# A decoder trunk on one core: a fourth seven-product block in each feed-forward layer, and the output pieces moved

## The chip, the core and the metric

The kernel runs on one core of one Trainium2 chip. The metric is device time in microseconds, measured over the whole launch. The median of three runs of the kernel before is 1028.6 us (1028.21, 1028.6 and 1033.28).

## The reference

The kernel computes a small decoder trunk for 256 tokens of width 1024: two layers, each with a feed-forward layer, a mixer and another feed-forward layer, and a residual with LayerNorm after each. The first mixer is a sparse attention, the second a state-space scan. The change touches the four feed-forward layers alone:

```python
D_MODEL = 1024
SEQ = 256
D_FF = 2816

def swiglu_ffn(x, w_in, w_out):
    gate, up = jnp.split(x @ w_in, 2, axis=-1)
    return (jax.nn.silu(gate) * up) @ w_out

# for each of the two layers i
x = layer_norm(DEEPNORM_ALPHA * x + 0.5 * swiglu_ffn(x, ffn1_w_in[i], ffn1_w_out[i]), ...)
m = mixer(x)
x = layer_norm(DEEPNORM_ALPHA * x + m, ...)
x = layer_norm(DEEPNORM_ALPHA * x + 0.5 * swiglu_ffn(x, ffn2_w_in[i], ffn2_w_out[i]), ...)
```

## The kernel before, in words

**Numbers.** Every operand of a large product is held as two halves: a rounded high part (H) and the rest, the low part (L). A product is three matmuls, H by H, H by L and L by H (`mm3`, L534 to L537).

**Weights.** The host cuts all weights into tiles of 128 x 1024 numbers (512 KB) and lays them in one array in the order of their use. A planner, the class `Weights` (L209), loads them in that order through SP's queue (`load`) and turns each into a unit, a high part by ScalarE (`make`, L329) and a low part by VectorE (`lows`, L357). At most ten units exist at once (`SLOTS`), and 7 or 9 raw tiles (`W.raws`). The order of the instructions on each engine is the order in which the program writes them. Each step of the program calls `pump` (L371), which makes up to n more units. VectorE's work is kept as a debt in columns (`owe`), and each product of TensorE takes 2400 off it (`product`, L263). Above a debt of 2500 (`MOST`), `pump` goes on only until the made units are six ahead of the used ones.

**A feed-forward layer** (`ffn`, L740). The 2816 gate columns and 2816 up columns are cut into 22 column blocks of 128 each, numbered j = 0 to 21. One layer goes through these parts:

- *Wide* (blocks 0 to 3): for both halves of the tokens, gate and up columns of two blocks are one product of 512 columns with the tokens on the output's partitions. Results lie in banks from `pmm()` (two banks in turn), in the first layer of the kernel the second pair in banks from `ptr()` (two in turn). `glu` (L775) takes silu of the gate half on ScalarE, and VectorE multiplies by the up half, which it reads in PSUM. `tr` (L764) then transposes on TensorE, ScalarE rounds (hH, L772) and VectorE splits off the low part (hL, L773).
- *One-block steps* (`one`, L872), R4 to R7: one column block at a time, a projection for the gate and one for the up columns (`proj_w`, lines L684 and L686), with the columns on the partitions, so that no transposes are needed.
- *Seven-product blocks* (`seven`, L903), S8, S12 and S16: four column blocks at once. The tokens are cut in two halves and the 1024 inputs in two halves, which makes a 2 x 2 by 2 x 2 block product; it is done with seven products in place of eight (A11, Q1, Q4, S2, S3, A12, A22), each four `mm3` of 512 columns. For this some weight tiles are added to others first (`sum`), by VectorE (L296) or by an accumulating DMA that POOL issues (L269), and so are input halves (`XT.sums`, L557, eight steps). ScalarE copies partial results out of PSUM and VectorE combines them; then comes `glu` as above.
- R20 and R21, one-block steps again.
- *Output pieces* (`out_pieces`, L848): one row block of the second weight matrix for all tokens, twelve matmuls into four banks (`acc`). Piece j can come when the hidden block j is split. Before, pieces 0 and 1 follow R6 and R7; four each lie in the slots of S8, S12 and S16; 14 and 15 follow R20 and R21.
- *Tail* (L695): the last six pieces, 16 to 21, for the first token half and then for the second, with the two LayerNorms.

Work that must wait is put off by steps: `later(f, d)` queues f for the d-th step from now, and `step` runs what is due and then pumps.

`ffn_steps` (L69) is the list of these parts, from which both the host's order of the weights (`ffn_units`, L83) and the device program are made.

Of the kernel before, what the change touches and what calls it, by code (L numbers as in the profile page):

```python
# [10 lines left out]
F32 = mybir.dt.float32  # L11
# [10 lines left out]
NJ = FF // 128  # L22
# [39 lines left out]

WIDE = 2
LAG = 6
SEVEN = (8, 12, 16)
MOST = 2500


def ffn_steps():  # L69


    steps, j, o = [], 2 * WIDE, 0
    while j < NJ:
        kind, n = ('S', 4) if j in SEVEN else ('R', 1)
        j += n
        outs = list(range(o, min(o + 4, max(o, j - LAG))))
        o += len(outs)
        steps.append((kind, j - n, outs))
    assert o == NJ - LAG, o
    return steps  # L80


def ffn_units(ws, wi, wo, wide, lag):  # L83
    def colblk(c0):
        return wi[:, c0:c0 + 128]

    def ktile(blk):
        n = blk.shape[1]
        return blk.reshape(DK, 128, n).transpose(1, 0, 2)

    def out_unit(j):
        ws.append(wo[j * 128:(j + 1) * 128])

    for w in range(wide):
        j = 2 * w
        blk = np.concatenate([wi[:, j * 128:(j + 2) * 128], wi[:, FF + j * 128:FF + (j + 2) * 128]], axis=1)
        t = ktile(blk)
        for k in range(0, DK, 2):
            ws.append(t[:, k:k + 2].reshape(128, -1))
    def quarter(j, kh):  # L100

        blk = np.concatenate([wi[:, j * 128:(j + 2) * 128], wi[:, FF + j * 128:FF + (j + 2) * 128]], axis=1)
        t = ktile(blk)
        return [t[:, k:k + 2].reshape(128, -1) for k in (4 * kh, 4 * kh + 2)]

    for kind, j, outs in ffn_steps():
        if kind == 'S':
            outs = outs + [None] * (4 - len(outs))

            def out():  # L110
                o = outs.pop(0)
                if o is not None:
                    out_unit(o)

            b11 = [ws.append(a) for a in quarter(j, 0)]
            b12 = [ws.raw(a) for a in quarter(j + 2, 0)]
            for i in range(2):
                ws.sum(b11[i], b12[i])
            out()
            b22 = [ws.append(a) for a in quarter(j + 2, 1)]  # L120
            for i in range(2):
                ws.sum(b11[i], b22[i])
            out()
            for i in range(2):
                ws.sum(b12[i], b22[i], True)
            b21 = [ws.append(a) for a in quarter(j, 1)]
            out()
            for i in range(2):
                ws.sum(b11[i], b21[i], True)
            out()  # L130
        else:
            ws.append(ktile(colblk(j * 128)).reshape(128, -1))
            ws.append(ktile(colblk(FF + j * 128)).reshape(128, -1))
            for o in outs:
                out_unit(o)
    for j in range(NJ - lag, NJ):
        out_unit(j)
# [276 lines left out]
def trunk_kernel(ctx: ExitStack, tc: tile.TileContext, widths, forms, x, ln_g, ln_b, wts, kvg, convp,  # L414
                 dt_bias, a_log, d_skip, norm_g, out):
    nc = tc.nc
# [5 lines left out]
    psum = ctx.enter_context(tc.tile_pool(name="psum", bufs=1, space=bass.MemoryType.PSUM))  # L422
# [4 lines left out]
    def nm(s):  # L427
        cnt[0] += 1
        return f"{s}_{cnt[0]}"
# [32 lines left out]
    def ptr():  # L462
        return psum.tile([128, 512], F32, name=nm("ptr"), tag="ptr", bufs=2)
# [276 lines left out]
    def ffn(xT, u0, ln_i, first=False, last=False, ff=False):  # L740
# [9 lines left out]
        def later(f, d=1):  # L750

            while len(queue) < d:
                queue.append([])
            queue[d - 1].append(f)
# [8 lines left out]

        def tr(t, w, h):  # L764

            pt = psum.tile([128, 512], F32, name=nm("pht"), tag=f"acc1{t}", bufs=1) if w < WIDE else ptr()
            for i in range(2):
                nc.tensor.transpose(pt[:, i * 128:(i + 1) * 128], h[:, i * 128:(i + 1) * 128], ident)
            v = pt[:, :256].rearrange("p (j t) -> p j t", j=2)
            sl = (slice(None), slice(None), slice(t * 128, (t + 1) * 128))  # L770
            H, L = [a[w].rearrange("p (j t) -> p j t", j=2)[sl] for a in (hH, hL)]
            nc.scalar.copy(H, v)  # L772
            return lambda: nc.vector.tensor_sub(L, v, H.bitcast(F32))  # L773

        def glu(t, w, c, sil=None):  # L775


            g, h = (c[:, :256], c[:, 256:]) if sil is None else (sil, f1("h"))
            nc.scalar.activation(g, c[:, :256], AF.Silu)

            def mul():
                nc.vector.tensor_mul(h, c[:, 256:], g)
                W.owe(800)
                later(lambda: later(tr(t, w, h)), 4 if w < WIDE and not first else 2)

            later(mul)

# [3 lines left out]
        if first:  # L791
# [3 lines left out]
            for w in range(WIDE):  # L795
# [15 lines left out]
                    glu(t, w, ps[t], f1("sil"))  # L811
                if not w:
                    for i in range(8):
                        later(lambda i=i: xT.sums(i), 1 + i)
        else:
            for t in range(2):
                for w in range(WIDE):
# [85 lines left out]
        def seven(j, outs):  # L903


            outs = outs + [None] * (4 - len(outs))

            def out():
                o = outs.pop(0)
                if o is not None:  # L910
                    out_pieces([o])

            w = j // 2
            for i in (w, w + 1):
# [789 lines left out]
    xT = XT(True)  # L1704
# [42 lines left out]
```

## Time and profile before

| | |
|---|---|
| runs, median | 1028.6 us (1028.21 to 1033.28) |
| span of the profiled execution | 1026.9 us, 1.7 us under the median of the runs; the profile gives no other time of its own |
| TensorE, matmuls busy | 1012.5 us, 99% |
| TensorE, weight loads busy | 861.4 us, 84% |
| VectorE busy | 869.6 us, 85% |
| ScalarE busy | 640.4 us, 62% |
| GpSimd busy | 107.7 us, 10% |
| granted TensorE clock, mean | 0.999 |

In the profile PE is TensorE's matmuls, PEld its weight loads, DVE VectorE, ACT ScalarE, POOL GpSimd and SP the queue that issues the weight loads from memory. A row of a group names the line, the engine, the operation, the tiles it writes and reads, the shape and the count; after the bar stand the busy time in us, the mean of one instruction in ns and the idle time of the engine before them with what ended it. A row of a timeline gives the start in us from the beginning of the span, the length in us, the engine, line and tiles, and in brackets the idle time before it. The length of a TensorE row includes the pipeline, so the distance between starts tells the pace.

### The profile page before, as it was taken

The numbers are of one execution on the slowest core, as the hardware profiler recorded it, in microseconds if no ns is written. First come the engines' busy times: TensorE is split into PE (matmuls) and PEld (weight loads), VectorE is DVE, ScalarE is ACT, GpSimd is POOL, SyncE is SP. The second block draws the span as 40 slices with busy tenths as digits, with TensorE's granted clock in tenths as the row PEclk, the third lists the DMA queues.
The fourth block names the chain that finished last, engine by engine and source line by source line (L and its number), as shares of the span: only waits on it lengthen the run. The fifth ranks groups of instructions, "written<-read, shape, count | busy, mean of one in ns | idle before, by whom it ended". The sixth has DMA issues, their size and how long they took to land.

```text
span 1026.9 us, 14872 instructions
## 1 busy us (share of the span) xinstructions
PE 1012.5 (99%) x5423; PEld 861.4 (84%) x5423; DVE 869.6 (85%) x1284; ACT 640.4 (62%) x978; POOL 107.7 (10%) x163
## 2 busy tenths in 40 slices
PE   9999999999999999999999999999999999999996
PEld 7888888888788888888888888999899888888885
DVE  6789997789789799878979887788999888898884
ACT  6666675476657666744766674486876547566660
POOL 2011000100010010001001000150111110101101
PEclk9999999999999999999999999999999999999999
DMA  9768998352657677983867797367775556679741
GB/s 335 284 143 285 270 321 303 104 170 77 200 188 243 174 207 242 333 321 123 246 185 195 240 338 277 124 170 242 206 219 191 190 219 226 147 233 285 214 186 41
DMA packets 62361, 223.32 MB, mean 217 GB/s; under 512 B 7024, under 2 KB 7088, under 8 KB 62288
## 3 DMA queue, kind: packets, MB, share of 16 engines
q1 hardware_dynamic: 51264, 183.43, 50.1%
q0 software_dynamic: 10736, 38.43, 18.2%
q8 instruction: 42, 0.69, 0.3%
q10 hardware_dynamic: 288, 0.52, 0.1%
q14 instruction: 31, 0.25, 0.1%
HBM read 193.48 MB, written 1.08 MB: 189 GB/s over the span
## 4 chain that ended last, share of the span: by engine, by line
PE 81%; DVE 9%; DMA 4%; issue 2%; ACT 2%; POOL 1%; POOLq 0%; DVEq 0%; ACTq 0%
PE pmm L537 9%; PE pmm L535 9%; PE pmm L536 9%; PE acc L535 8%; PE acc L537 8%; PE acc L536 8%; DVE wl L357 5%; PE ptr L684 4%; PE pmm L684 4%; DMA raw<-raw 4%; PE ptr L686 2%; PE pmm L686 2%; PE pxs L535 2%; PE pxs L537 1%; PE pxs L536 1%
## 5 line engine op out<-in xcount | busy, mean ns | idle before, releaser
L357 DVE TENSOR_TENSOR wl<-raw,wh 128x1024 fp32r<-128x1024 f32 (+2 forms) x399 | 469.1, 1212 | 15.6 <-ACT wh L329 15.1
L329 ACT CAST wh<-raw 128x1024 fp32r<-128x1024 f32 (+2 forms) x406 | 407.5, 1044 | 107.7 <-DVE raw L296 46.6
L535 PE MATMUL acc<-wh,hH 128*128 128x512 f32 (+1 forms) x352 | 137.7, 391 | 0.0
L537 PE MATMUL acc<-wh,hL 128*128 128x512 f32 (+1 forms) x352 | 136.7, 388 | 0.0
L536 PE MATMUL acc<-wl,hH 128*128 128x512 f32 (+1 forms) x352 | 136.7, 388 | 0.0
L535 PE MATMUL pmm<-wh,xT 128*128 128x512 f32 (+2 forms) x288 | 115.0, 399 | 0.0
L537 PE MATMUL pmm<-wh,xT 128*128 128x512 f32 (+2 forms) x288 | 111.7, 388 | 0.1
L536 PE MATMUL pmm<-wl,xT 128*128 128x512 f32 (+2 forms) x288 | 111.0, 385 | 0.0
L269 POOL DMA_DIRECT2D raw<-raw x48 | 41.6, 867 | 439.5 <-DVE raw L296 148.6
L537 PEld LDWEIGHTS acc<-wh,hL 128*128 128x128 f32 x352 | 66.1, 188 | 13.7
L535 PEld LDWEIGHTS acc<-wh,hH 128*128 128x128 f32 x352 | 66.2, 188 | 12.8
L536 PEld LDWEIGHTS acc<-wl,hH 128*128 128x128 f32 x352 | 66.2, 188 | 12.6
L537 PE MATMUL pmm<-wh,xf 128*128 128x512 f32 x192 | 74.8, 390 | 0.0
L535 PE MATMUL pmm<-wh,xf 128*128 128x512 f32 x192 | 74.7, 389 | 0.0
L536 PE MATMUL pmm<-wl,xf 128*128 128x512 f32 x192 | 74.7, 389 | 0.0
L537 PEld LDWEIGHTS pmm<-wh,xT 128*128 128x128 f32 x288 | 54.4, 189 | 12.4 <-DVE xT L532 1.4
L536 PEld LDWEIGHTS pmm<-wl,xT 128*128 128x128 f32 x288 | 54.7, 190 | 9.7 <-DVE wl L357 0.3
L535 PEld LDWEIGHTS pmm<-wh,xT 128*128 128x128 f32 x288 | 54.6, 190 | 9.1
L296 DVE TENSOR_TENSOR raw<-raw,raw 128x1024 f32<-128x1024 f32 x48 | 57.9, 1220 | 0.4
L684 PE MATMUL pmm<-xT,wh 128*128 128x512 f32 x192 | 49.3, 399 | 0.0
L684 PE MATMUL ptr<-xT,wh 128*128 128x512 f32 x192 | 48.0, 392 | 0.0
L535 PE MATMUL pxs<-xT,wh 128*128 128x256 f32 x160 | 46.4, 290 | 0.0
(313 smaller groups left out, 1903.5 us busy)
## 6 DMA issues: line engine op xcount, KB each, us to landing
raw<-in_wts_dram SPq DMA_DIRECT2D x339, 512.0 KB, 5.2
raw<-raw POOLq DMA_DIRECT2D x48, 512.0 KB, 5.8
M<-scr POOLq DMA_DIRECT2D x8, 512.0 KB, 5.5
lng<-in_ln_g_dram POOLq DMA_DIRECT2D x6, 512.0 KB, 5.4
lnb<-in_ln_b_dram POOLq DMA_DIRECT2D x6, 512.0 KB, 6.3
wl<-raw POOLq DMA_DIRECT2D x5, 512.0 KB, 5.6
raw<-in_wts_dram SPq DMA_DIRECT2D x4, 408.0 KB, 5.3
out_dram<-x SPq DMA_DIRECT2D x4, 256.0 KB, 2.1
```

The costliest lines, as they stand in the source:

```text
L269: self.nc.gpsimd.dma_start(self.raw[r], self.raw[other], accum_op=ALU.add)
L296: self.nc.vector.tensor_add(self.raw[r], self.raw[r], self.raw[other])
L329: nc.scalar.copy(h[:, c:c + n], raw[:, c:c + n])
L357: self.nc.vector.tensor_sub(lo[:, s], raw[:, s], h[:, s].bitcast(F32))
L535: nc.tensor.matmul(ps, lh, rh, start=first, stop=False, skip_group_check=on)
L536: nc.tensor.matmul(ps, lh, rl, start=False, stop=False, skip_group_check=on)
L537: nc.tensor.matmul(ps, ll, rh, start=False, stop=last, skip_group_check=on)
L684: nc.tensor.matmul(ps, H[:, k * 128:(k + 1) * 128], xT.HL[:, k, :], start=k == 0, stop=False)
L686: nc.tensor.matmul(ps[:, :SEQ], L[:, k * 128:(k + 1) * 128], xT.H[:, k, :], start=False, stop=k == DK - 1)
```

## The change

The step list gets a fourth seven-product block, S4, in place of R4 to R7. The four blocks now stand in a row straight after the wide part. Every block has four output pieces in its four slots: S4 pieces 0 to 3, each later block j the pieces j-2, j-1, j-4 and j-3, which are the hidden blocks of the block before it. R20 and R21 have none. The tail keeps its six.

Five smaller edits go with it. In `tr`, the second pair of wide blocks uses the `ptr` banks for the second token half, and for both halves in the first layer. In `glu`, when the result still lies in a matmul bank (the last product of a block, A22), ScalarE copies the up half to SBUF behind its silu, and VectorE multiplies from there. The transposes of the wide results of the second token half come two steps after the multiply and no longer four. In the first layer the eight steps of `XT.sums` come two per step. And the lists of output pieces hold lists.

```diff
-SEVEN = (8, 12, 16)
+SEVEN = (4, 8, 12, 16)
 MOST = 2500

 def ffn_steps():
-    steps, j, o = [], 2 * WIDE, 0
-    while j < NJ:
-        kind, n = ('S', 4) if j in SEVEN else ('R', 1)
-        j += n
-        outs = list(range(o, min(o + 4, max(o, j - LAG))))
-        o += len(outs)
-        steps.append((kind, j - n, outs))
-    assert o == NJ - LAG, o
+    steps = []
+    for j in SEVEN:
+        steps.append(('S', j, [[j - 2], [j - 1], [j - 4], [j - 3]] if j > SEVEN[0] else [[0], [1], [2], [3]]))
+    steps += [('R', j, []) for j in range(SEVEN[-1] + 4, NJ)]
     return steps
...
         def tr(t, w, h):
-            pt = psum.tile([128, 512], F32, name=nm("pht"), tag=f"acc1{t}", bufs=1) if w < WIDE else ptr()
+            pt = psum.tile([128, 512], F32, name=nm("pht"), tag=f"acc1{t}", bufs=1) if w < WIDE - (t or first) else ptr()
...
             g, h = (c[:, :256], c[:, 256:]) if sil is None else (sil, f1("h"))
             nc.scalar.activation(g, c[:, :256], AF.Silu)
+            if sil is not None and w >= WIDE:
+                nc.scalar.copy(h, c[:, 256:])

             def mul():
-                nc.vector.tensor_mul(h, c[:, 256:], g)
+                nc.vector.tensor_mul(h, h if w >= WIDE else c[:, 256:], g)
                 W.owe(800)
-                later(lambda: later(tr(t, w, h)), 4 if w < WIDE and not first else 2)
+                later(lambda: later(tr(t, w, h)), 2 if first or t or w >= WIDE else 4)
...
                     for i in range(8):
-                        later(lambda i=i: xT.sums(i), 1 + i)
+                        later(lambda i=i: xT.sums(i), 1 + i // 2)
...
         def seven(j, outs):
-            outs = outs + [None] * (4 - len(outs))
+            outs = list(outs)

             def out():
-                o = outs.pop(0)
-                if o is not None:
-                    out_pieces([o])
+                out_pieces(outs.pop(0))
```

More of the change, by code (lines that the diff above doesn't have):

```diff
@@ L107, in ffn_units @@
         if kind == 'S':
-            outs = outs + [None] * (4 - len(outs))
+            outs = list(outs)
             def out():
-                o = outs.pop(0)
-                if o is not None:
+                for o in outs.pop(0):
                     out_unit(o)
@@ L903, in seven @@
         def seven(j, outs):
-            outs = outs + [None] * (4 - len(outs))
+            outs = list(outs)
             def out():
-                o = outs.pop(0)
-                if o is not None:
-                    out_pieces([o])
+                out_pieces(outs.pop(0))
             w = j // 2
```

## The prediction

> **What bounds the kernel now.** I read the page first.
>
> ```profile
> span 1026.9 us, 14872 instructions
> PE 1012.5 (99%) x5423; PEld 861.4 (84%) x5423; DVE 869.6 (85%) x1284; ACT 640.4 (62%) x978; POOL 107.7 (10%) x163
> ...
> PE 81%; DVE 9%; DMA 4%; issue 2%; ACT 2%; POOL 1%; POOLq 0%; DVEq 0%; ACTq 0%
> ...
> L357 DVE TENSOR_TENSOR wl<-raw,wh 128x1024 fp32r<-128x1024 f32 (+2 forms) x399 | 469.1, 1212 | 15.6 <-ACT wh L329 15.1
> L329 ACT CAST wh<-raw 128x1024 fp32r<-128x1024 f32 (+2 forms) x406 | 407.5, 1044 | 107.7 <-DVE raw L296 46.6
> ...
> L269 POOL DMA_DIRECT2D raw<-raw x48 | 41.6, 867 | 439.5 <-DVE raw L296 148.6
> ...
> L296 DVE TENSOR_TENSOR raw<-raw,raw 128x1024 f32<-128x1024 f32 x48 | 57.9, 1220 | 0.4
> ```
>
> TensorE works all the time, and VectorE is second, mostly with the low halves of the weights (L357) and the sums that seven-product blocks need (L296). A mean says little here, so I cut the feed-forward layers into stretches. In the windows view the columns after the length are busy time and count on TensorE, its weight loads, VectorE, ScalarE, GpSimd, then the granted clock, the DMA share and GB/s. The first row is R4 to R7 (the one-block steps for column blocks 4 to 7) of layer 1, the next two are its last two seven-product blocks; then R4 to R7, the last block, and R20 with R21 of layer 3.
>
> ```profile
> core 0: us, PE busy (x) PEld busy (x) DVE busy (x) ACT busy (x) POOL busy (x), PEclk, DMA share, GB/s
> 31.84:60.07 28.23, 28.23 (x157) 24.61 (x156) 25.20 (x41) 17.66 (x32) 1.80 (x2) 1.00 0.65 206
> 90.38:121.31 30.93, 30.93 (x143) 25.52 (x142) 29.64 (x34) 22.03 (x31) 3.46 (x4) 1.00 0.92 272
> 121.31:152.27 30.96, 30.96 (x143) 25.52 (x142) 29.62 (x35) 23.55 (x32) 2.61 (x3) 1.00 0.94 278
> 492.89:521.01 28.12, 28.12 (x157) 24.49 (x156) 26.58 (x38) 17.45 (x31) 1.78 (x2) 1.00 0.68 204
> 582.30:613.20 30.90, 30.90 (x143) 25.52 (x142) 27.65 (x32) 23.73 (x33) 1.74 (x3) 1.00 0.85 269
> 613.20:628.50 15.30, 14.66 (x84) 12.59 (x82) 14.10 (x19) 10.10 (x16) 1.10 (x2) 1.00 0.97 346
> ```
>
> Every stretch but the last is TensorE from end to end. Its only wait inside the feed-forward layers is in the view of waits, at R20 in three layers, 2.0 us in all:
>
> ```profile
> PE ptr L768 <- DVE hL L773: 2.0, 3, 1.1
> ```
>
> How tight VectorE is shows in the second row above. That stretch, asked for line L357 alone and then for L296 alone:
>
> ```profile
> 90.38:121.31 30.93, 21.00 (x18) 1.00 0.92 272
> ...
> 90.38:121.31 30.93, 4.79 (x4) 1.00 0.92 272
> ```
>
> Eighteen lows and four sums are the whole load of a block with four output pieces. So a full block takes VectorE 29.64 of TensorE's 30.93 us, 1.17 us a low (21.00/18) and 1.20 a sum. Two such blocks in a row ran there without a wait on TensorE.
>
> **What is removed and added on TensorE.** From the timeline, R4's two projections, four transposes and what follows them, and the first matmuls of two products one after the other:
>
> ```profile
> 31.84 1.98 PE L684 MATMUL pmm<-xT,wh 128*128 128x512 f32 x8
> ...
> 34.60 2.00 PE L684 MATMUL pmm<-xT,wh 128*128 128x512 f32 x8
> ...
> 40.19 0.60 PE L768 MATMUL pht<-ident,h 128*128 128x128 f32 x4
> 40.55 2.10 PE L684 MATMUL ptr<-xT,wh 128*128 128x512 f32 x8
> ...
> 60.07 0.39 PE L535 MATMUL pmm<-wh,xT 128*128 128x512 f32 x1
> ...
> 62.79 0.39 PE L535 MATMUL pmm<-wh,xf 128*128 128x512 f32 x1
> ```
>
> A product or an output piece, each 12 matmuls, takes 62.79 - 60.07 = 2.72 us; a projection 34.60 - 31.84 = 2.76, eight of them 22.1. From the windows: 28.23 less two output pieces of 2.72 is 22.8, and 40.55 - 40.19 = 0.36 of that are transposes which stay, so 22.4. The block that comes instead takes 30.95 less its four output pieces (10.9) = 20.05; it holds seven products (19.0) and its own transposes (1.0). The output pieces only move. That is **2.4 us less in each of four layers, 9.5 in all**.
>
> **What is added elsewhere, and what hides it.** Fourteen weight forms replace eight: six more lows (6 x 1.17) and eight sums, four by VectorE (4 x 1.20) and four by accumulating DMAs issued on POOL (0.87 each). The combinations, multiplies and splits roughly cancel those of R4 to R7. That is 12 us more on VectorE and 6 x 1.04 = 6 more on ScalarE per layer. The loads on SP keep their number (eight tiles of 512 KB for four column blocks in either form); only the output pieces' tiles come in another order. ScalarE is idle a quarter of a block, and POOL's 108 us leave it idle nearly always. VectorE's 12 us find 1.3 us per block and its idle time in the tail; the second row shows a block in that state running at TensorE's pace. If that cover fails, see rival B. The copy of the up half by ScalarE costs 0.37 us in each of 16 blocks (by the 256-column copies):
>
> ```profile
> L887 ACT COPY h<-pmm 128x256 f32<-128x256 f32 x12 | 4.5, 374 | 6.3 <-PE pmm L686 6.2
> ...
> L782 DVE TENSOR_TENSOR c<-c 128x256 f32<-128x256 f32 x36 | 15.0, 417 | 0.0
> ...
> L782 DVE TENSOR_TENSOR h<-pmm,sil 128x256 f32<-128x256 f32 x26 | 10.8, 418 | 2.1 <-ACT sil L779 2.1
> ```
>
> It frees the bank for the next block's first product without VectorE. The transposes of the second token half come two steps earlier and into another bank; TensorE does as many. The multiply itself gets no cheaper: 417 ns from SBUF, 418 from PSUM. [...] The two rows show 1 ns, so I count nothing.*
>
> **The wait at R20.** In layer 1, whose blocks run with the weights only some six units ahead, there is none; in the other layers, which come out of R4 to R7 far ahead, ScalarE casts a form far ahead before it empties a bank, and VectorE waits for the bank's copy and falls behind:
>
> ```profile
> 605.02 0.69 DVE L926 TENSOR_TENSOR c<-c 128x512 f32<-128x512 f32 x1 [2.15 <-ACT c L949]
> ```
>
>  After the change all layers enter their blocks without that lead and should run like layer 1. I count half of the 2.0 us: **1.0 less**; bounds 0 and 2.0.
>
> **The start of the first block, layer 1.** The eight steps that sum the input halves (L557) now fall two at a time into the last 11 us of the wide part, and Q1's two weight sums with them. VectorE and ScalarE before:
>
> ```profile
> 23.32 0.75 DVE L782 TENSOR_TENSOR h<-pmm,sil 128x256 f32<-128x256 f32 x2
> ...
> 25.30 0.68 DVE L574 TENSOR_TENSOR xq<-xq,pxT 128x512 f32<-128x512 f32 x1
> ...
> 26.62 1.22 DVE L357 TENSOR_TENSOR wl<-raw,wh 128x1024 fp32r<-128x1024 f32 x1
> 30.69 1.23 DVE L357 TENSOR_TENSOR wl<-raw,wh 128x1024 fp32r<-128x1024 f32 x1 [2.85 <-ACT wh L329]
> ...
> 29.07 0.65 ACT L772 CAST hH<-pht 128x256 fp32r<-128x256 f32 x2 [1.71 <-PE pht L768]
> ```
>
> ScalarE's rounding of one input half:
>
> ```profile
> L566 ACT CAST xf<-xq 128x512 fp32r<-128x512 f32 x16 | 9.6, 619 | 1.9 <-DVE xq L574 0.9 <-DVE xq L587 0.8
> ```
>
> In program order VectorE has, from 24.1: two steps of 0.69, a low, three of 0.69, a sum; that is 28.7 to 29.9 with ScalarE's roundings (0.62) between. ScalarE's high (1.05) and the low (1.17) give Q1's first unit at 32.1. ScalarE then rounds hH and S2 (0.65 + 0.62), VectorE does two steps and the second sum (to 34.75), high and low follow: Q1's second unit at 36.9. TensorE wants it at 31.84 + 2.72 + 1.36 = 35.9: 1.0 late. The same queue then holds two splits, a step and the low of output piece 0 (39.5 against 38.3: 1.2 late), and two multiplies, two sums and the low of Q4 (1.3 late). That is 3.5 at most when every step is as long as taken, 0 if the planner's order is looser: I take **3.0**.
>
> **The start in layers 2 to 4.** The second product, Q1, writes the bank that holds the last wide result. That bank is freed by a VectorE multiply, which ends at 495.2, with the next user at 495.76:
>
> ```profile
> 494.76 0.42 DVE L782 TENSOR_TENSOR h<-pmm,sil 128x256 f32<-128x256 f32 x1
> ...
> 495.76 2.00 PE L684 MATMUL pmm<-xT,wh 128*128 128x512 f32 x8
> ```
>
> Ahead of it come two sums (2.4) and one split more (0.33); the planner counts them as debt and puts two lows behind it (2.3). So it ends at about 495.6 to 496.0, and Q1 wants the bank at 492.89 + 2.72 = 495.6: 0.4 each, **1.2** in all (0 to 4, if the lows stay ahead in half the cases).
>
> **The end.** R20 and R21 lose the output piece that followed each, so the tail starts 2.72 us sooner after R21, and its sixth piece needs R21's result 5 x 0.68 (three matmuls, 2.72/4) = 3.4 us after R21's last matmul. Layer 3 now, with that matmul at 628.5:
>
> ```profile
> 629.10 0.42 DVE L888 TENSOR_TENSOR h<-ptr,h 128x256 f32<-128x256 f32 x1 [1.12 <-ACT h L887]
> 629.45 1.00 DVE L357 TENSOR_TENSOR wl<-raw,wh 128x816 fp32r<-128x816 f32 x1
> 630.36 0.42 DVE L891 TENSOR_TENSOR h<-h,gate 128x256 f32<-128x256 f32 x1
> ...
> 632.70 0.43 DVE L894 TENSOR_TENSOR hL<-h,hH 128x256 fp32r<-128x256 f32 x1 [1.29 <-ACT hH L893]
> ```
>
> The split ends 4.6 us after it, against 2.72 + 3.4 = 6.1 now and 3.4 to 3.9 then. So 0 to 1.2 late in each layer, depending on how many lows stand between; I take the middle, 0.6, **2.4** in all. The LayerNorm behind it has its work unchanged.
>
> **The sum.** -9.5 - 1.0 + 3.0 + 1.2 + 2.4 = -3.9. It is made against the span of 1026.9, which gives 1023.0. The median of the runs is 1028.6, 1.7 above that span, and I carry the 1.7: **1024.7**, -0.4%. With every unknown at its good end it is -11.5 (1017.1), at its bad end -9.5 + 3.5 + 4 + 4.8 = +2.8 (1031.4).
>
> **Rivals.**
>
> A: the new waits are covered. The planner's order makes units earlier than I walked, as the unhurried rows at R4 now suggest, and the R20 waits go: -9.5 - 2.0 = 1017.1, or with one or two short waits up to 1023. For it: no stretch now shows TensorE waiting for a weight. Against: VectorE was back to back from 23.3 to 27.8 in layer 1 (the rows above), and its 2.85 us of wait there was ScalarE's, behind TensorE's transposes; this order puts more in front of Q1.
>
> B: VectorE paces the blocks, which is slower. By counts and single means a block holds 18 x 1.212 + 4 x 1.220 + 3 x 0.69 + 8 x 0.417 = 32.1 us, over TensorE's 30.95, and with no R4 to R7 between there is no lead to live on. Sixteen blocks at 1.2 more are +18.4, less 11.5: about +7, 1035.5. It decides from a block of 31.7 us on, where 16 x 0.7 eats the gain. Against it: back to back, instructions overlap, and the second window row holds that very load in 29.64. [...] The trace disagrees so far: 2.72 us per 12 matmuls without a gap.*
>
> C: DMA eats the gain. Blocks run the DMA engines at 0.92 to 0.94 in layer 1; four accumulates more per layer land later, ScalarE waits for them, then everything behind it. One us per block of the sixteen gives -11.5 + 16 = +4.5 at worst, near 0 likelier: 1028. Against it: 12 x 512 KB of weights and four sums per block are in those rows already.
>
> **How the numbers follow.** A measurement of this kernel can tell about 0.5%, 5.1 us, from no change, so faster is below 1023.5. My forecast has 0.50 (own range 1021.5 to 1029; a tenth of it below 1023.5), A 0.36, B 0.07, C 0.07. Faster: 0.36 + 0.05 = 0.41. Within 0.5%: 0.45 + 0.07 = 0.52. Slower: 0.07. The range takes in A's end and the bad end of the sum, and leaves out B: 1017 to 1031.
>
> **What would show it.** Windows of each block must be near 31 us with some 143 matmuls and transposes, and the projections' L684 must fall to a third, 128 matmuls of 384. In the view of waits, TensorE waiting for L357, L773 or a multiply at L782 right after the wide part is my start; for L894 or L357 at the tail's sixth piece my end. None of them means A. Block windows over 31.7 with VectorE at 97% or more mean B; ScalarE waiting for the accumulate at blocks that lengthen means C. I am wrong if blocks 2 to 4 in a row differ from layer 1's 30.95.

## The result, and the profile after

The changed kernel takes 1034.9 us (median; 1034.3 to 1035.5), the kernel before 1028.7. The ratio is 1.0053, with a 95% interval of 1.0038 to 1.0068: slower by half a per cent, where 1024.7 (1017 to 1031) was forecast. The profiled executions have spans of 1026.9 and 1032.6 us, so 5.7 us are to be found. Head of the page of the changed kernel and three of its groups; lines up to `glu` and again from `seven` on are numbered 5 lower than before, those between them 3, so L352 is the low half of a weight, L291 VectorE's weight sum, L264 the accumulating DMA:

```profile
span 1032.6 us, 14723 instructions
...
PE 1005.6 (97%) x5279; PEld 847.3 (82%) x5279; DVE 910.1 (88%) x1304; ACT 665.2 (64%) x1002; POOL 121.4 (12%) x179
...
L352 DVE TENSOR_TENSOR wl<-raw,wh 128x1024 fp32r<-128x1024 f32 (+2 forms) x423 | 495.5, 1214 | 14.0 <-ACT wh L324 13.5
...
L264 POOL DMA_DIRECT2D raw<-raw x64 | 55.4, 865 | 451.6 <-DVE raw L291 253.6
...
L291 DVE TENSOR_TENSOR raw<-raw,raw 128x1024 f32<-128x1024 f32 x64 | 77.0, 1220 | 0.2
```

TensorE has 6.9 us less to do and is busy 97% of the time, no longer 99%. VectorE has 40.5 more. The view of waits of the changed kernel, TensorE's rows inside the feed-forward layers (waited in all, times, longest):

```profile
PE acc L531 <- DVE wl L352: 5.1, 5, 1.1
PE pht L763 <- DVE hL L768: 4.2, 3, 1.4
PE pmm L531 <- DVE wl L352: 1.7, 2, 1.1
...
PE ptr L763 <- DVE hL L768: 1.2, 2, 0.6
...
PE pxT L548 <- DVE x L637: 0.7, 2, 0.4
```

Before, TensorE waited 2.2 us there: 2.0 at R20, which are gone, and 0.2 of the last row. Now it is 12.9 us, all of them for VectorE. Blocks of layer 3, windows of the changed kernel (columns as in the prediction): S4, S8, S12, S16, then R20 with R21.

```profile
498.59:529.18 30.59, 30.59 (x139) 25.22 (x138) 26.78 (x28) 19.73 (x27) 1.71 (x2) 1.00 0.84 257
529.18:560.96 31.78, 31.16 (x143) 25.51 (x142) 30.80 (x36) 23.47 (x35) 4.28 (x5) 1.00 0.90 265
560.96:591.92 30.96, 30.96 (x143) 25.53 (x142) 29.63 (x34) 22.27 (x33) 3.44 (x4) 1.00 0.92 271
591.92:622.83 30.91, 30.91 (x143) 25.54 (x142) 29.48 (x35) 24.14 (x34) 2.58 (x3) 1.00 0.95 283
622.83:634.54 11.71, 11.71 (x72) 10.36 (x71) 7.85 (x12) 6.16 (x11) 1.10 (x2) 1.00 0.86 300
```

Three blocks of four run at TensorE's pace; only S8 waits (31.78 less 31.16 us; one such wait in layer 2 too, 0.55). So the blocks themselves did what was forecast. The time went to the two ends of the row. Cutting both traces at the same instructions gives this ledger, in us, summed over the four layers:

| stretch | before | after | difference |
|---|---|---|---|
| start to the first R4/S4 of layer 1 | 31.84 | 31.02 | -0.8 |
| R4/S4 to the tail | 137.58, 137.95, 138.33, 138.75 | 138.60, 135.84, 135.95, 135.31 | -6.9 |
| wide part, layers 2 to 4 | 23.95, 23.63, 23.62 | 25.70, 25.50, 25.32 | +5.3 |
| tail to the next layer (or last matmul) | 17.27, 17.24, 17.26, 16.69 | 18.93, 19.43, 18.66, 18.09 | +6.7 |
| attention and SSD layers | 294.74 | 294.85 | +0.1 |
| last matmul to the end | 8.01 | 9.36 | +1.4 |

The second row holds the waits at the start of layer 1 (+2.9) and at S8 (+1.6) and the lost waits at R20 (2.6 with the gaps around them). Without these, the products saved 6.9 + 2.9 + 1.6 - 2.6 = 8.8 us. The first row is no gain: the first twelve matmuls of the wide part, the same in both kernels, took 4.33 us before (7.04 to 11.37, where the next transposes start) and 3.30 after (7.25 to 10.55), and over the kernels below the same wide part ended up to 1.6 us earlier or later.

**The wide part.** VectorE of the changed kernel in layer 2, from the timeline, and under it the transposes that wait for it on TensorE (in brackets the wait):

```profile
307.37 1.23 DVE L291 TENSOR_TENSOR raw<-raw,raw 128x1024 f32<-128x1024 f32 x1
...
311.57 1.22 DVE L291 TENSOR_TENSOR raw<-raw,raw 128x1024 f32<-128x1024 f32 x1
312.71 0.42 DVE L768 TENSOR_TENSOR hL<-pht,hH 128x256 fp32r<-128x256 f32 x1
```

```profile
313.18 0.44 PE L763 MATMUL pht<-ident,h 128*128 128x128 f32 x2 [1.40 <-DVE hL L768]
```

Two weight sums for S4 now stand in this queue, and the split of the first wide result (L768) behind them. It starts 4.05 us after that result's transposes (308.66 on TensorE). Before, it came 1.57 us after them (306.61):

```profile
308.18 0.42 DVE L773 TENSOR_TENSOR hL<-pht,hH 128x256 fp32r<-128x256 f32 x1
```

The 2.5 us between are the two sums, and the next wide result's transposes want the bank. With the gaps around it the wait costs 1.56 us a layer, 4.7 of the 5.3 in the ledger.

**The tail.** Windows of layer 2, R20 with R21 (before, with their two output pieces) and the tail; first the kernel before, then the changed one:

```profile
434.38:452.02 17.64, 17.38 (x95) 14.85 (x94) 16.15 (x22) 12.08 (x19) 1.09 (x2) 1.00 0.99 386
452.02:469.26 17.24, 17.24 (x82) 14.34 (x80) 11.84 (x16) 6.65 (x8) 1.30 (x2) 1.00 0.44 148
```

```profile
441.96:453.66 11.70, 11.70 (x71) 10.35 (x70) 7.85 (x12) 6.16 (x11) 1.09 (x2) 1.00 1.00 396
453.66:473.09 19.43, 17.90 (x82) 14.27 (x81) 17.34 (x22) 11.41 (x15) 1.30 (x2) 1.00 0.65 206
```

VectorE had 5.4 us to spare in the tail; now it has 2.1, and TensorE waits 1.5. In the timeline of the tail, first before, then after:

```profile
454.02 1.22 DVE L357 TENSOR_TENSOR wl<-raw,wh 128x1024 fp32r<-128x1024 f32 x1
456.32 0.69 DVE L618 SCALAR_TENSOR_TENSOR x<-acc,x 128x512 f32<-128x512 f32 x1 [1.08 <-PE acc L537]
```

```profile
457.08 0.42 DVE L891 TENSOR_TENSOR hL<-h,hH 128x256 fp32r<-128x256 f32 x1 [0.58 <-ACT hH L890]
457.43 5.76 DVE L352 TENSOR_TENSOR wl<-raw,wh 128x1024 fp32r<-128x1024 f32 x5
463.10 0.68 DVE L613 SCALAR_TENSOR_TENSOR x<-acc,x 128x512 f32<-128x512 f32 x1
```

Where one low stood behind R21's split, five do: that of the sixth piece's own weight, for which TensorE waits, and four for the next layer, ahead of the LayerNorm. ScalarE makes the high halves of these five only after R21's last matmul:

```profile
454.76 1.99 ACT L324 CAST wh<-raw 128x1024 fp32r<-128x1024 f32 x2
456.95 2.94 ACT L324 CAST wh<-raw 128x1024 fp32r<-128x1024 f32 x3
```

**The end.** Rows of the line that ends the program, kernel before, then after (count, then ns shortest/median/longest):

```profile
L1743 POOLq DRAIN  x3: 46/102/4947, 1021.0 to 1026.6; - x3
```

```profile
L1738 POOLq DRAIN  x3: 46/102/6419, 1025.3 to 1032.3; - x3
```

GpSimd's closing drain lasts 1.47 us longer and is now what ends last: at 1025.3 + 6.42 = 1031.8 us, where SP's own drain, behind the output's stores, starts at 1030.1.

### The profile page after: what moved, and what is told of

Its sections match the earlier page's. It is cut to its first block, busy times and chain, and to the rows that moved or that the text cites. A ratio compares the mean times of both kernels' runs of the same rounds, so it can differ in the third digit from the quotient of the medians.

```text
span 1032.6 us, 14723 instructions
## 1 busy us (share of the span) xinstructions
PE 1005.6 (97%) x5279; PEld 847.3 (82%) x5279; DVE 910.1 (88%) x1304; ACT 665.2 (64%) x1002; POOL 121.4 (12%) x179
## 4 chain that ended last, share of the span: by engine, by line
PE 76%; DVE 12%; issue 5%; DMA 4%; ACT 2%; POOL 1%; POOLq 0%; SPq 0%; DVEq 0%; ACTq 0%
PE pmm L532 10%; PE pmm L530 10%; PE pmm L531 10%; PE acc L530 8%; PE acc L531 8%; PE acc L532 8%; DVE wl L352 5%; DVE raw L291 2%; DMA raw<-raw 2%; PE pxs L530 1%; PE pxs L532 1%; PE pxs L531 1%; PE pmm L679 1%; PE ptr L679 1%; PE ptr L763 1%
## 5 line engine op out<-in xcount | busy, mean ns | idle before, releaser
L352 DVE TENSOR_TENSOR wl<-raw,wh 128x1024 fp32r<-128x1024 f32 (+2 forms) x423 | 495.5, 1214 | 14.0 <-ACT wh L324 13.5
L324 ACT CAST wh<-raw 128x1024 fp32r<-128x1024 f32 (+3 forms) x430 | 430.4, 1047 | 95.6 <-DVE raw L291 46.0
L530 PE MATMUL pmm<-wh,xT 128*128 128x512 f32 (+2 forms) x320 | 128.0, 400 | 0.0
L532 PE MATMUL pmm<-wh,xT 128*128 128x512 f32 (+2 forms) x320 | 123.8, 387 | 0.4 <-DVE xT L527 0.4
L531 PE MATMUL pmm<-wl,xT 128*128 128x512 f32 (+2 forms) x320 | 123.2, 385 | 0.0
L264 POOL DMA_DIRECT2D raw<-raw x64 | 55.4, 865 | 451.6 <-DVE raw L291 253.6
L531 PE MATMUL pmm<-wl,xf 128*128 128x512 f32 x256 | 99.9, 390 | 1.7 <-DVE wl L352 1.7
L530 PE MATMUL pmm<-wh,xf 128*128 128x512 f32 x256 | 100.1, 391 | 0.0
L532 PE MATMUL pmm<-wh,xf 128*128 128x512 f32 x256 | 99.8, 390 | 0.0
L291 DVE TENSOR_TENSOR raw<-raw,raw 128x1024 f32<-128x1024 f32 x64 | 77.0, 1220 | 0.2
L531 PEld LDWEIGHTS pmm<-wl,xf 128*128 128x128 f32 x256 | 48.1, 188 | 12.4 <-DVE wl L352 2.5
L532 PEld LDWEIGHTS pmm<-wh,xf 128*128 128x128 f32 x256 | 48.1, 188 | 10.0
L530 PEld LDWEIGHTS pmm<-wh,xf 128*128 128x128 f32 x256 | 48.1, 188 | 9.8
```

What stands on the lines that cost most here:

```text
L264: self.nc.gpsimd.dma_start(self.raw[r], self.raw[other], accum_op=ALU.add)
L291: self.nc.vector.tensor_add(self.raw[r], self.raw[r], self.raw[other])
L324: nc.scalar.copy(h[:, c:c + n], raw[:, c:c + n])
L352: self.nc.vector.tensor_sub(lo[:, s], raw[:, s], h[:, s].bitcast(F32))
L530: nc.tensor.matmul(ps, lh, rh, start=first, stop=False, skip_group_check=on)
L531: nc.tensor.matmul(ps, lh, rl, start=False, stop=False, skip_group_check=on)
```

## The experiments

Theories: **L** (also called theory C, which is not the prediction's rival C), every wait is local, a cover lost at one place, and repairing it gains what the wait shows; **V**, VectorE has too much to do at both ends of the row, and a repaired wait comes back nearby. Each kernel was timed beside the kernel before, and ratios are to that. It took 1028.7 to 1029.1 us beside the first twelve kernels of the table and 1029.3 to 1030.1 beside the last six; these are compared by their ratios, of which 0.1% is 1.03 us.

| kernel | us | ratio | 95% interval |
|---|---|---|---|
| changed | 1034.9 | 1.0053 | 1.0038 to 1.0068 |
| bank | 1032.2 | 1.0030 | 1.0018 to 1.0042 |
| two pieces to R20, R21 | 1035.3 | 1.0058 | 1.0044 to 1.0072 |
| sums by DMA | 1050.8 | 1.0209 | 1.0195 to 1.0224 |
| no copy | 1034.7 | 1.0058 | 1.0045 to 1.0071 |
| piece eleventh | 1033.3 | 1.0044 | 1.0031 to 1.0056 |
| one piece to R21 | 1040.2 | 1.0115 | 1.0099 to 1.0130 |
| layer 1 as before | 1031.1 | 1.0021 | 1.0011 to 1.0031 |
| bank, eleventh | 1030.9 | 1.0024 | 1.0014 to 1.0034 |
| piece ninth | 1033.0 | 1.0039 | 1.0026 to 1.0052 |
| bank, ninth | 1030.8 | 1.0017 | 1.0007 to 1.0028 |
| bank, ninth, layer 1 | 1027.6 | 0.9985 | 0.9975 to 0.9994 |
| ninth, lows behind LayerNorm | 1045.3 | 1.0144 | 1.0127 to 1.0161 |
| ninth, lows off VectorE | 1029.9 | 0.9997 | 0.9985 to 1.0010 |
| bank, ninth, layer 1, lows behind | 1040.2 | 1.0099 | 1.0084 to 1.0114 |
| bank, layer 1, lows behind | 1045.8 | 1.0155 | 1.0138 to 1.0172 |
| bank, ninth, layer 1, lows off | 1024.2 | 0.9953 | 0.9938 to 0.9967 |
| bank, ninth, lows off | 1027.6 | 0.9982 | 0.9974 to 0.9991 |

### Another bank for the wide transposes

```diff
-            pt = psum.tile([128, 512], F32, name=nm("pht"), tag=f"acc1{t}", bufs=1) if w < WIDE - (t or first) else ptr()
+            pt = psum.tile([128, 512], F32, name=nm("pht"), tag=f"acc1{t}", bufs=1) if w < WIDE - 1 else ptr()
```

> The changed kernel, with one bank different: in layers 2 to 4 the transposes of the wide result (first token half, second block) go to a ptr bank and no longer wait until VectorE has split the result before it out of the same bank. Theory L (each new wait is local: a cover was lost at one place, and nothing behind it is late): the wait of 4.2 us in three layers at these transposes goes, and the time falls from 1034.9 by 4.2 to 4.7 us, to about 1030.4. Rival V (VectorE simply has too much work from the wide part on, the bank is only where it shows first): the 1.4 us come back a few us later as waits for a low or a multiply in the first seven-product block, and the time stays within 1.5 us of 1034.9.

It gained 2.7 us of the 4.2 to 4.7. The row of the bank is gone from the waits, and a shorter one stands for all transposes:

```profile
PE ptr L763 <- DVE hL L768: 1.0, 3, 0.4
```

Of the 1.56 us in layer 2, 0.26 came back at the transposes after and 0.26 at Q1's bank, where the prediction had looked for the wait; at S8 0.88 are left, in layers 3 and 4 too. Somewhat more than half is L, the rest V.

### The two sums by DMA

```diff
-                ws.sum(b11[i], b12[i])
+                ws.sum(b11[i], b12[i], j == 4)
```

> The changed kernel, with the two weight sums in front of the first block (b11+b12 for S4) made by accumulating DMAs instead of VectorE, in all four layers; the planner's debt, which counts only VectorE's sums, is smaller by them, so lows may move ahead too. Theory L: the two sums of 1.22 us stand ahead of the split of the first wide result on VectorE and are what makes it late; without them the waits of 1.4 to 1.56 us in the wide part of layers 2 to 4 go (about -4.5 us), and of the 2.9 us at the start of layer 1 some half (-1.5), if the DMAs (5.8 us from issue to landing) are issued early: 1029 to 1031. Rival V: two sums are 2.4 of VectorE's 230 us in a layer, the lag remains, 1033 to 1035. A late DMA would show as ScalarE waiting for it and TensorE for the high half behind it.

Both missed. Without the sums the split is on time again, 1.54 us after its transposes (311.51), so the sums were all of its delay. But ScalarE now waited for the accumulating DMAs, its silu came late, and behind that the multiply, for which the transposes waited 0.85 to 1.1 us in place of 1.56. VectorE and ScalarE, and two windows of that kernel (behind the five engines stands the granted clock):

```profile
313.05 0.42 DVE L768 TENSOR_TENSOR hL<-pht,hH 128x256 fp32r<-128x256 f32 x1
316.73 0.42 DVE L779 TENSOR_TENSOR h<-pmm,sil 128x256 f32<-128x256 f32 x1 [3.26 <-ACT sil L774]
```

```profile
315.37 1.05 ACT L324 CAST wh<-raw 128x1024 fp32r<-128x1024 f32 x1 [3.06 <-DMA raw<-raw]
```

```profile
322.00:326.00 4.00, 1.11 (x5) 0.57 (x4) 4.00 (x6) 1.89 (x4) 0.00 (x0) 1.00 0.48 112
326.00:330.00 4.00, 3.06 (x9) 2.41 (x10) 2.01 (x3) 0.00 (x0) 0.00 (x0) 0.71 0.80 224
```

TensorE waited 4.0 us at Q1 in each of three layers, for the multiply that frees its bank, and in the second window ran at a granted clock of 0.71.

### Without ScalarE's copy

```diff
-            if sil is not None and w >= WIDE:
-                nc.scalar.copy(h, c[:, 256:])
...
-                nc.vector.tensor_mul(h, h if w >= WIDE else c[:, 256:], g)
+                nc.vector.tensor_mul(h, c[:, 256:], g)
```

> The changed kernel without the copy of the up half by ScalarE: VectorE multiplies straight from the bank after a block's last product. Theory L: the copy costs ScalarE 0.37 us in each of 16 blocks off the path and lets the next block's first product have its bank without VectorE; without it TensorE waits at the blocks' first products only if VectorE is more than about 11 us behind, which no view shows: within 1 us of 1034.9. Rival V: VectorE is that far behind, and 12 block starts wait for the bank, 0.5 to 1 us each: 1041 to 1047.

As L had it: no difference clear of noise, and nearly the same waits. The multiply takes 424 ns from SBUF and 417 from PSUM in the changed kernel.

### Layer 1 as before

```diff
-    for kind, j, outs in ffn_steps():
+    for kind, j, outs in ffn_steps(first):
```

with R4 to R7, the old bank and one sum per step in layer 1 (the same in the list of units).

> The changed kernel, with layer 1 put back to R4 to R7 and three blocks, its transposes' bank and its sums one per step as before; layers 2 to 4 as changed. Theory: in layer 1 the change gave 1.9 us of products and took 2.9 of waits at the block's start and 1.3 at the tail, so putting it back gains 1.0 + 1.3 = 2.3; four accumulating DMAs fewer shorten GpSimd's closing drain, 0.093 us for each by three runs (4.95 us with 53 accumulating DMAs in all, 6.42 with 69, 7.19 with 77), by 0.37: the drain lasts 6.05 us. Together about 1032.2. If the start of layer 1 is not where the time goes (its first matmuls start up to 1 us earlier or later from run to run, as the weights land), within 0.7 of 1034.9. If the drain has nothing to do with those DMAs it stays at 6.4.

3.7 us gained, more than the 2.7 named; the drain lasted 6.01 us, as forecast. In layer 1 the change, with its tail and its drain, had cost more than it saved.

### The tail: pieces moved, order changed

Two output pieces, then one, from the last block to behind R20 and R21:

```diff
+    steps[-1][2][2:] = [[], []]
-    steps += [('R', j, []) for j in range(SEVEN[-1] + 4, NJ)]
+    steps += [('R', j, [j - 8]) for j in range(SEVEN[-1] + 4, NJ)]
```

> The changed kernel, with output pieces 12 and 13 taken out of the last seven-product block and put behind R20 and R21, one each, as cover. The work is the same. Theory L: the sixth piece of the tail no longer waits for the low half of R21's result, 1.3 us in each of four layers; the time falls by about 5 us, to 1029.7, perhaps 1 us less if R20's first split is late again. Rival V (VectorE is behind at the tail because of its load over the whole layer): the wait at the sixth piece keeps at least half of its 1.3 us, and the time is not under 1032.

```diff
+    steps[-1][2][3:] = [[]]
-    steps += [('R', j, []) for j in range(SEVEN[-1] + 4, NJ)]
+    steps += [('R', j, [13] if j == NJ - 1 else []) for j in range(SEVEN[-1] + 4, NJ)]
```

> The changed kernel, with only output piece 13 moved from the last block to behind R21; R20 keeps none. Theory C: the last block is shorter by one piece of 2.72 us and not by two, so the wait at R20's transposes, 0.95 us with two pieces moved, is under 0.4; the tail's wait goes; the time falls by 4 to 5 us, to about 1030. Rival V: the wait at R20 stays at 0.9 or so and the gain is 1.5 us at most: 1033.5.

With two moved, the tail's wait went and 0.95 us at R20 came: nothing gained clear of noise. With one moved both theories missed, by 5 us the other way. R21's first projection (L680) waits for a bank:

```profile
PE ptr L680 <- DVE hL L769: 7.1, 4, 1.8
```

An output piece is cover of 2.72 us and also one step of the queue that holds the block's late transposes; without it these come together in R20 and hold both ptr banks. That reading comes from the order in the trace; no run tests it by itself.

Then the order of the tail's pieces alone, R21's as eleventh or as ninth step of the first token half:

```diff
-        order = [[(i, hf) for hf in range(2) for i in range(n)],
+        k = n if hook else n - 1
+        order = [[(i, 0) for i in range(k)] + [(i, 1) for i in range(3)] + [(i, 0) for i in range(k, n)]
+                 + [(i, 1) for i in range(3, n)],
```

> The changed kernel, with the tail's order for the first token half altered: its last piece (R21's) comes as eleventh and twelfth step, behind both halves of the other five, and no longer as sixth. Same work, same weights, nothing moved in the blocks. Theory C (the tail's wait is a cover lost: R21's result is simply asked for 2.72 us sooner): the wait of 1.3 us goes in four layers and nothing takes its place, R20 included, and the time falls from 1034.9 by 5 us to about 1029.8. Rival V (VectorE is behind with its weights there, so that a low half is late wherever the piece stands; taking out cover moved the wait to R20 in the run before): the wait comes back at the second half or at the LayerNorm, and the time stays over 1033.

> The changed kernel, with the tail's last piece (R21's) in the first token half as ninth step and not as sixth: behind the other five of the first half and three of the second. TensorE then asks for R21's split 3 x 0.68 = 2.0 us later, which is more than the wait of 1.3, and the first output half is whole at 9 x 0.68 = 6.1 us, 2 us ahead of the second, so that the LayerNorm has its usual start (with the piece as eleventh step it was late, and the next layer's transposes waited 1.0 to 2.1 us for it). Theory C (a lost cover, at a known place): the wait of 1.3 us goes in four layers, the waits at the LayerNorm stay as in the changed kernel (0.4 and 0.6 us), the time falls from 1034.9 by 4 to 5 us, to 1030 to 1031. Rival V (VectorE's backlog sets the end of the tail, wherever the piece stands): the LayerNorm's waits grow by about as much, and the time stays over 1032.5.

1.6 and 1.9 us gained, not 5. The sixth piece no longer waits; the next layer's transposes do, in either form. Waits with the piece as ninth:

```profile
PE ptr L548 <- DVE x L637: 2.1, 3, 0.8
PE pxT L548 <- DVE x L637: 1.9, 3, 0.9
```

So at the tail V holds for both places tried: the LayerNorm's output is late. Combinations with the bank and layer 1 add up only so far:

> The changed kernel with both repairs: the ptr bank for the wide transposes of layers 2 to 4 (2.7 us gained alone) and R21's piece last in the tail's first half. Theory C: independent waits, the gains add up: 1034.9 - 2.7 - 5 = 1027.2, level with the kernel before (1028.7). Rival V: VectorE's 40 us of added work show again at another place, and the sum of both gains is under 4 us: over 1031.

> The repairs together: layer 1 with R4 to R7 as before, the ptr bank for the wide transposes of layers 2 to 4, and the tail's last piece as ninth step. Theory C: the gains add up, 1034.9 - 3.7 (layer 1, which holds one tail wait) - 2.7 (bank) - 3.9 (three tails) = 1024.6, faster than the kernel before by 0.4%. Rival V: they don't add up, 1028 or more.

> As the run before, but with the four blocks in a row in layer 1 too. Theory C: 1034.9 - 2.7 - 5 = 1027.2, 2.4 us slower than with layer 1 put back. Rival V: 1030.5 or more.

With the bank, the eleventh step gives 1030.9 and the ninth 1030.8 us, where both expectations had 1027.2 by C: the tail's gain is what is missing. With layer 1 put back too it is 1027.6, 0.15% faster than the kernel before; C had 1024.6 and V 1028 or more, so it lies nearer V.

### The five lows

Four of the five are for the next layer. They are put behind the LayerNorm; then, ahead of it, they are taken off VectorE. Both have the piece as ninth step.

```diff
         W.highs(8)
-        W.lows()
+        W.lows(0 if hook else sum(v >= u + n for v in W.late))
```

> The changed kernel, with the tail's last piece as ninth step (1033.0 alone), and the low halves of the next layer's first four units behind the LayerNorm of the first token half and no longer ahead of it. VectorE does the same work. Theory Q (they stand in the wrong place): the LayerNorm starts up to 4.6 us sooner, the waits of the next layer's transposes (1.0 to 2.1 us in three layers) go, the lows are done before their matmuls; the time falls by 3 to 4.5 us, to 1028.5 to 1030. Theory W (VectorE has too much work between the blocks' end and the next layer): the four lows delay the next splits of the input instead, TensorE waits there, and the gain is under 1.5 us: over 1031.5.

```diff
         gb = load_ln(ln_i)
+        if not last:
+            W.by_dma = set(range(u + LAG, u + LAG + 4))
```

> As the run before, but the four lows stay ahead of the LayerNorm and are taken off VectorE in layers 1 to 3: ScalarE writes the negative high half and an accumulating DMA adds the weight, as the kernel already does for five units. It relieves VectorE of 4.6 us in each of three tails and adds 4.2 us to ScalarE, which is idle for 5 us there, and 12 accumulating DMAs, which lengthen GpSimd's closing drain by 12 x 0.093 = 1.1 us. Theory W and theory Q alike: the LayerNorm is on time, the waits of 1.0 to 2.1 us go, -4.7 + 1.1 = about -3.6 from 1033.0, 1029.4; by W it is well below the run before, by Q level with it or a little above. If the DMAs land late, the next layer's first matmuls wait for a low half.

The second edit reached fewer lows than its expectation says: four behind layer 1 and three each behind layers 2 and 3, ten in all (VectorE has 1294 instructions, not 1304).

Against the kernel with the piece as ninth step, moving the lows cost 10.8 us; taking ten of them off VectorE gained 4.3, where about 3.6 were expected. Moved behind, they stood with three others ahead of the splits of the next layer's input. VectorE, TensorE and its wait, and TensorE's window after it:

```profile
472.29 8.03 DVE L352 TENSOR_TENSOR wl<-raw,wh 128x1024 fp32r<-128x1024 f32 x7
480.24 1.28 DVE L527 TENSOR_TENSOR xT<-pxT,xT 128x512 fp32r<-128x512 f32 x2
```

```profile
480.98 0.79 PE L532 MATMUL pmm<-wh,xT 128*128 128x512 f32 x1 [4.52 <-DVE xT L527]
```

```profile
481.50:485.00 3.50, 3.50 (x10) 2.65 (x9) 3.43 (x6) 0.00 (x0) 0.00 (x0) 0.50 0.73 263
```

Taken off, two lows are left behind R21's split in layer 2, and VectorE waits for TensorE again as it did before the change; the transposes' waits behind the LayerNorm fall from 4.0 us to 0.5:

```profile
457.04 2.36 DVE L352 TENSOR_TENSOR wl<-raw,wh 128x1024 fp32r<-128x1024 f32 x2
459.62 0.69 DVE L613 SCALAR_TENSOR_TENSOR x<-acc,x 128x512 f32<-128x512 f32 x1 [0.23 <-PE acc L532]
```

This speaks for theory W: in the tail VectorE has as much to do (17.34 us) as TensorE's work there lasted before (17.24), and neither of the two orders tried had room for it. That no order has is not shown: the same work cost 10.8 us more in one order than in the other, and the lows were not tried behind the splits of the input. The same on top of the version with the other repairs:

> The version of 1027.6 us (layer 1 with R4 to R7, the ptr bank for the wide transposes, the tail's last piece as ninth step) with the four low halves behind the LayerNorm. Theory Q: its waits at the transposes after layers 2 and 3 (1.1 + 1.0 and 1.0 us) go: 1024.5, faster than the kernel before by 0.4%. Theory W: within 1 us of 1027.6.

> As the run before, but with the tail's pieces in their old order, so that R21's piece is the sixth. The low half of its weight (a unit of this layer, first of the five on VectorE) still ends some 1.3 us late, so that wait stays in three layers; the LayerNorm is on time. About 3 x 1.3 = 3.9 us slower than the run before if the two are independent; if the LayerNorm has that much to spare, level with it.

The first is 11.7 us slower than without the edit: both theories missed, Q by 15 us and W, which had no change, by 12, since the same waits for the input came as above. The second is 5.8 us slower still, where 3.9 or nothing was expected. The wait for the sixth piece's own low is there again, 1.09 us in each of layers 2 to 4, though the other four lows are gone from ahead of the LayerNorm; what the remaining 2 us are stays open.

### All repairs

```diff
-        if not last:
+        if not (first or last):
```

with the ptr bank, the ninth step and layer 1 as before; then with four blocks in layer 1 too and the lows off VectorE in layers 1 to 3. Here too fewer lows are moved than expected, six and ten.

> The version of 1027.6 us (layer 1 with R4 to R7, the ptr bank for the wide transposes, the tail's last piece as ninth step), with the four low halves ahead of the LayerNorm taken off VectorE (ScalarE and accumulating DMAs) in layers 2 and 3, where that version waits 2.1 and 1.0 us. Theory W: those waits go, -3.1, and eight accumulating DMAs add 8 x 0.093 = 0.7 to the closing drain: 2.4 us faster than that version, whose ratio to the kernel before was 0.9985; about 0.996. If the waits come back at another place: 0.998 or more.

> As the run before, but with the four blocks in a row in layer 1 too, and the four lows off VectorE in layers 1 to 3. The start of layer 1 keeps its waits of 2.9 us, against 1.9 us of products that it saves and 4 accumulating DMAs more in its first block and 4 more in its tail (0.7 us of drain): 1.5 to 2.5 us slower than the run before, ratio 0.998. If layer 1's start costs nothing in the end: level with it.

As W had it: 1024.2 us, 0.47% faster than the kernel before (ratio 0.9953, 0.996 expected); with layer 1 changed as well it is 3.0 us slower, somewhat more than the 1.5 to 2.5 expected. The page of the former:

```profile
span 1022.5 us, 14779 instructions
...
PE 1006.9 (98%) x5315; PEld 850.8 (83%) x5315; DVE 894.0 (87%) x1293; ACT 664.3 (65%) x1005; POOL 122.6 (12%) x181
```

So with these repairs the block in place of R4 to R7 pays in three layers. VectorE has 16 us less to do than in the changed kernel: 10 by layer 1, as the run with layer 1 as before shows (899.9), and 6 by the six lows. No run gave the repairs to the kernel before; that one has no wait at the places they mend, but that the whole gain is the blocks' is argued, not shown.

## Why the prediction was wrong

The forecast was a sum of -3.9; the span's difference is +5.7.

| step, as the prediction put it | forecast | measured |
|---|---|---|
| products: 2.4 less in each of four layers | -9.5 | -8.8 |
| the wait at R20, half of it | -1.0 | -2.6 |
| the start of the first block, layer 1 | +3.0 | +2.9 |
| the start in layers 2 to 4 | +1.2 | +5.3, and +1.6 at S8 |
| the end (tail) | +2.4 | +6.7 |
| not counted: GpSimd's drain | 0 | +1.4 |
| start-up, other layers | 0 | -0.7 |

**Right:** the products, and that four blocks in a row keep TensorE's pace. The start of layer 1 came out to a tenth of a microsecond and where it was looked for: TensorE waits 0.64 us for the low of Q1's second unit, 0.74 for that of output piece 0 and 1.05 for that of Q4 (36.15, 38.55 and 42.61 in the timeline), 2.9 with the gaps. That it fits so closely is luck in part, since the prediction took 3.0 from a range of 0 to 3.5. The multiply was no cheaper from SBUF, as said (424 ns, 417 from PSUM).

**The rivals.** B, a block of 31.7 us with VectorE at 97%, is met by S8 alone, in layers 2 and 3 (30.80 of 31.78 us in layer 3). C has its sign there: ScalarE's waits for accumulating DMAs grew from 13.7 us (9 times) to 17.8 (19 times), and one stands in S4 of layer 3, ahead of a wait of VectorE:

```profile
518.68 1.05 ACT L324 CAST wh<-raw 128x1024 fp32r<-128x1024 f32 x1 [2.28 <-DMA raw<-raw]
520.25 0.69 DVE L921 TENSOR_TENSOR c<-c 128x512 f32<-128x512 f32 x1 [1.40 <-ACT c L944]
```

How much of S8's 1.6 us comes from it no run separates. The blocks behind S8 have no such loss.

**Wrong, "The start in layers 2 to 4".** It found the two sums and looked for who waits at the one place it had in mind, Q1's bank. The first waiter was another, in the part that the diff hardly touches: the transposes of the second wide result, whose single bank is freed by a split that now stands behind the sums. 1.56 us a layer there, not 0.4. Before, and in the run with the sums by DMA, the split came 1.57 and 1.54 us after its transposes, with VectorE's sums 4.05. The bank run showed that 0.88 us a layer can be had back and that the rest returns. With S8 it is 6.9 us against a range of 0 to 4.

**Wrong, "The end".** It allowed 0 to 4.8 us, and 6.7 came. It followed R21's split: that ended at 457.08 + 0.42, 3.8 us after the tail's start at 453.66, sooner than the 4.6 it used, and nearly in time. What TensorE waited for was the low half of that piece's weight, behind the split, and behind it came four more, which the LayerNorm waited for. The sentence "the LayerNorm behind it has its work unchanged" held, but its engine's queue didn't. The two output pieces had given 5.4 us of TensorE's time in which VectorE made such lows; "its idle time in the tail", by which the prediction covered VectorE's added work, was spent by moving them. The runs bear it out: with three or four of the four lows off VectorE the LayerNorm is on time, and the piece's own low costs its 1.09 us with or without them as long as the piece is the sixth. That the lows couldn't be made sooner, in R20 and R21 where VectorE idles for 3.9 of 11.7 us, fits ScalarE's rows above (the five highs start at 454.76); the program's ten slots would explain it (six for the tail, four that come free only with R20's and R21's units), but no run tested that.

**Not counted:** GpSimd's drain, 1.4 us, which the prediction put at nothing.

The prediction had the right kind of loss, but the measured 5.7 lies beyond its bad end of +2.8, since both ends and the drain exceed what it allowed. It treated the two ends as independent, while both come, as far as the runs show, from VectorE's 40 us more, placed where it had least room. Its other reading, that eighteen lows and four sums are a block's whole load on VectorE, is wrong too (21.00 + 4.79 = 25.8 of 29.64 us), but no term uses it. The prediction turned rival B down because the blocks ran without a gap; in the tail of layer 2 the rival's reading held: VectorE was busy for 17.34 of 19.43 us, TensorE's weight loads for 14.27, and TensorE waited for VectorE.

## What to carry to other kernels

Check the spare time of the second engine stage by stage, and most of all in the stage from which work is moved away: an output piece there was the time in which another engine caught up. When an operation is put into a queue, list every instruction behind it until the next idle gap, and who waits for each; the first waiter may be in code that the change does not touch. When a repaired wait comes back elsewhere, try taking work off the engine; here that gained where both reorderings fell short.

## What the runs showed of the hardware

GpSimd's closing drain was longer in the kernels whose programs had issued more accumulating DMAs: 4.95 us with 53 of them, 6.01 with 65, 6.42 with 69 (6.417 to 6.421 in four kernels). In the changed kernel the last was issued at 974.5 us and none took more than 9.9 us to land, while the drain began at 1025.3. The kernel with its sums by DMA has 77:

```profile
L1738 POOLq DRAIN  x3: 46/93/7195, 1040.8 to 1048.5; - x3
```

That is 0.089 to 0.094 us for each one over the 53. In the kernel before, the drain ended at 1021.00 + 4.95 = 1025.95 us, when SP's own, behind the output's stores, began (1026.0); in the changed kernel it ended 1.7 us after SP's began. The run with layer 1 put back forecast 6.05 us by this and measured 6.01.

TensorE ran slower behind its longest waits. In the kernel with the piece as ninth step and the lows behind the LayerNorm it waited 4.52 us in layer 2; the next 3.5 us show a granted clock of 0.50 and ten matmuls, where a product's 12 in 2.72 us would give fifteen. In layer 1 of that kernel it did nothing from 188 to 192 us, and 192 to 196 ran at 0.50 too. With the sums by DMA it worked for 1.11 of the 4 us from 322 to 326, and ran at 0.71 from 326 to 330 and at 0.73 in the 2 us behind. Behind shorter waits both were seen. The changed kernel stayed at 1.00 behind the 1.09 us at the sixth piece in layer 2. The kernel with one piece at R21 waits 1.78 us in all four layers; in layer 3 the next 2 us ran at 1.00, and in layer 2 at 0.51:

```profile
449.70:452.00 2.30, 2.30 (x6) 1.84 (x7) 0.18 (x1) 0.00 (x0) 0.28 (x1) 0.51 0.98 394
```

What decides between the two no run here shows.
